# Four seven-product pairs in each half of the long w_down passes, three residues by DMA, and a load queue that follows the buffers

## The chip, the cores and the metric

The kernel runs on one core of one Trainium2 chip. The metric is device time in microseconds (us). Before the change three runs gave 1047.63, 1048.29 and 1048.34 us, so the median is 1048.29 us. Every engine of the core works through its own queue in order: PE multiplies matrices, PEld is the part of PE that loads the standing operand, DVE and ACT do arithmetic on vectors, POOL here does little more than issue DMAs, and SP issues DMAs.

## The reference

One layer of an encoder with sequence 256 and width 2048, all in float32:

```
xn   = rms_norm(x);  q, k, v, ga, gg = split(xn @ w_in)          # w_in 2048 x 5120
att  = differential attention(q, k, v), 4 heads, chunk mask, then rms_norm
u    = silu(layer_norm(causal depthwise conv(ga * sigmoid(gg))))
h    = x + concat(att, u) @ w_out                                 # w_out 2048 x 2048
hn   = rms_norm(h)
out  = h + (silu(hn @ w_gate) * (hn @ w_up)) @ w_down             # 2048 x 5632, twice; 5632 x 2048
```

The last line is some two thirds of the time. It has 5632 hidden columns, which the kernel takes as eleven blocks of 512.

## The kernel before, in words

**Precision.** A float32 number is kept as two parts: a rounded one, `hi`, and what is left, `lo` (the residue). A product of two such numbers takes three matmuls: hi by hi, lo by hi, hi by lo. The rounding is done by ACT (`round_chunk`, L320), the residue by DVE (`split_chunk`, L329). For some chunks the residue is made "by DMA" instead: ACT writes the negative of the raw numbers into `lo` (L323), and POOL issues a DMA that adds the raw numbers in a rounding form onto it (L324).

**Work units.** The last line of the reference runs as a list of chunks, `chunks`. A chunk of kind `g` or `u` (a *two*) covers two tiles of 128 rows and one stretch of 512 columns, and takes 12 matmuls (`multiply_two`, L1014, L1015, L1020). A chunk of kind `s` (a *pair*) covers two tiles of rows and two stretches of columns at once, by the seven products of Strassen's scheme in Winograd's form: 7 x 3 = 21 matmuls where plain work takes 24 (`multiply_pair`, L993 to L995). For a pair the weights must first be combined: `round_pair` makes four sums on DVE (L966 to L968) and rounds the raw ones on ACT (L969); `split_pair` rounds the sums on ACT (L972) and makes the seven residues on DVE (L975, L976). The seven combinations of the other operand are made once (`make_forms` for the gate and up blocks, `make_down_forms` for the passes over w_down).

**Blocks and passes.** Eleven blocks fall in three groups, `FGROUPS = (4, 4, 3)`. A block (but for block 0, which is done plainly) has twelve chunks in the order `ORDER = "sggsggsuusuu"`: 4 pairs and 8 twos. After a group comes its pass over w_down (`down_pass`): two halves, each for 1024 output columns. A pass after four blocks has 16 row tiles; each half takes them as `ND` = 2 pairs and 12 twos, in the orders of `DORDERS[4]`; the short last pass has 12 row tiles, 2 pairs and 8 twos a half. In this text the chunks of a block or a half are called seats 0, 1, 2 and so on.

**Order of the work.** `run_chunks` writes the program in one pass over the chunks: before it writes the matmuls of chunk t it writes the loads and the rounding of chunk t + 3 and the residue of chunk t + 2. The loads of pairs are written six chunks ahead (`PAIR_AHEAD`). Loads go by SP's queue, in the order written, and each waits until its buffer is free: five buffers for twos (`RAW_BUFS`), two for pairs (`wb`). All else (sums of the products, the transposed activations, the combinations for w_down) is written by small generators that are taken one step further at fixed points: four times in a pair, twice in a two (`resume`). `lag(n)` puts n such steps between two parts of a generator.

**The end of a block.** `bank_sums` combines seven PSUM banks on DVE (L1092 to L1099) after the last pair. `block_done` adds the last two banks after the last chunk (L1113), multiplies (L1115), and after a lag of four steps `transposed` has PE transpose the result (L831), ACT round it (L840) and DVE make the residue (L842). In the first two blocks of a group the first two row tiles are kept raw (`raw_act`), for the seven combinations of the pass. `make_down_forms` makes these, one or two instructions every five steps, during the third and fourth block of the group (L868 to L888).

**The end of a half.** `down_half` and `down_whole` add the sums to `hd`, the running sum in memory, by adding DMAs from POOL (L1138, L1155). In the very last half the sums are added on the core and written out.

Of the kernel before, what the change touches and what calls it, by code (L numbers as in the profile page):

```python
# [88 lines left out]
ND = 2  # L89
DORDERS = {4: ("gguuggsguugsuu", "sgggugggusuuuu"), 3: ("gguusggsuu", "gggsgsuuuu")}  # L90
# [8 lines left out]
PAIR_AHEAD = 6  # L99
# [23 lines left out]
def tile_block(  # L123
# [263 lines left out]
    def run_chunks():  # L387
        n = len(chunks)
        i = j = p = 0
        behind = [k for k in range(n) if chunks[k].get("kind") == "s"][NS]  # L390
        for t in range(n):
            hi_lead, lo_lead = lead(t)
            while j < min(i, t + 1 + lo_lead):
                chunks[j]["split"](chunks[j])
                j += 1
            while p < min(n, t + 1 + PAIR_AHEAD):
                if chunks[p].get("kind") == "s":

                    if p < behind and p > t + hi_lead:
                        break  # L400
                    load_pair(chunks[p])
                p += 1
            while i < min(n, t + 1 + hi_lead):
                if i in before:
                    before[i]()
                chunks[i]["load"](chunks[i])
                chunks[i]["round"](chunks[i])
                i += 1
                if hi_lead == lo_lead:
                    chunks[j]["split"](chunks[j])  # L410
                    j += 1
            while j < min(n, t + 1 + lo_lead):
                chunks[j]["split"](chunks[j])
                j += 1
            chunks[t]["multiply"](chunks[t])
# [405 lines left out]
    def transposed(j, aa):  # L821
        last = j + 1 in FIRSTS
        b = j - group_of(j)[1]
        for t in range(N // P // 2):
# [20 lines left out]
            yield from lag(1 if last else 4)  # L845
# [12 lines left out]
    def make_down_forms(g):  # L858

        fp = ffn["pool"]  # L860
        gap = lambda: lag(5 if FGROUPS[g] == 4 else 2)
        a11, a21 = (raw_act[0][:, :, m * P : (m + 1) * P] for m in range(NM))
        a12, a22 = (raw_act[1][:, :, m * P : (m + 1) * P] for m in range(NM))

        hi = fp.tile([P, 7, ND, P], F32R, tag="dhi", name="dhi")
        lo = fp.tile([P, 3, ND, P], F32R, tag="dlo", name="dlo")
        fa, fb = (lhs.tile([P, 2, ND, P], F32, tag=t, name="dsums") for t in ("lhi", "llo"))
        act.copy(hi[:, 0], a11)  # L868
        dve.scalar_tensor_tensor(fa[:, 0], a21, -1.0, a22, ALU.mult, ALU.subtract)
        yield from gap()  # L870
        act.copy(hi[:, 1], a12)
        dve.scalar_tensor_tensor(fa[:, 1], fa[:, 0], -1.0, a11, ALU.mult, ALU.subtract)
        yield from gap()
        act.activation(hi[:, 2], a22, AF.Copy, scale=-1.0)
        dve.tensor_tensor(fb[:, 0], a11, a21, ALU.subtract)
# [8 lines left out]
        dve.scalar_tensor_tensor(lo[:, 2], a22, -1.0, hi[:, 2].bitcast(F32), ALU.mult, ALU.subtract)  # L884
        yield from gap()
        pairs = [lhs.tile([P, 2, ND, P], F32R, tag=t, name="dlo2") for t in ("lhi", "llo")]
        for i, f in ((0, fa), (1, fb)):
            dve.tensor_tensor(pairs[i], f, hi[:, 3 + 2 * i : 5 + 2 * i].bitcast(F32), ALU.subtract)  # L888
            yield from gap()
# [357 lines left out]
```

## Time and profile before

| | us |
|---|---|
| profiled execution, device time | 1048.92 |
| its span on the core | 1047.1 |
| median of three runs | 1048.29 |
| PE busy in the span | 1036.2 |
| DVE busy | 900.6 |
| ACT busy | 621.6 |
| the long pass of the second group, both halves (768.74 to 854.15) | 85.41 |

The span is what the core's instructions cover, and the device time of the same execution is 1.8 us longer. Busy time of PE overlaps itself, because matmuls are pipelined: a matmul is shown with some 0.39 us, while the next one starts 0.23 us after it. Stretches of the span are therefore read by the starts of chunks.

### The profile page before, as it was taken

Reading aid. Unit: us, or ns where it says so; the run is one execution under the profiler, and the core shown is the slowest. Engines: PE = TensorE matmul, PEld = TensorE weight load, DVE = VectorE, ACT = ScalarE, POOL = GpSimd, SP = SyncE. Lnnn points to the kernel's source line nnn. Section 1 sums busy time; section 2 is a strip of 40 time slices with the busy share of each in tenths; the row PEclk is TensorE's granted clock in tenths of the full one; section 3 lists DMA queues with packets and bytes.
Section 4 is the critical chain, followed back from the end, with each engine's and each line's share of the span. In section 5 each row is a group of like instructions: output and inputs, shape, how many; then the busy total and the mean of one; then the engine's idle time right before and its main releaser. Section 6 shows DMA issues by size and latency. Waiting matters only on the chain.

```text
span 1047.1 us, 12933 instructions
## 1 busy us (share of the span) xinstructions
PE 1036.2 (99%) x4663; PEld 852.5 (81%) x4663; DVE 900.6 (86%) x1095; ACT 621.6 (59%) x786; POOL 100.5 (10%) x143
## 2 busy tenths in 40 slices
PE   9999999999999999999999999999999999999998
PEld 7888887877788788888888888888888888888886
DVE  7899889898765599999787898999878789989897
ACT  7544666755756565776463657666644446657442
POOL 0130122201100100000001010000000110000010
PEclk9999999999999999999999999999999999999999
DMA  9657654453546566987867789879757879798683
GB/s 335 227 182 280 212 163 167 154 181 134 177 153 226 194 223 214 268 266 236 232 210 188 217 271 273 256 217 285 248 175 241 219 208 291 222 287 267 187 265 85
DMA packets 113936, 231.30 MB, mean 221 GB/s; under 512 B 7504, under 2 KB 8656, under 8 KB 113616
## 3 DMA queue, kind: packets, MB, share of 16 engines
q1 hardware_dynamic: 104864, 203.71, 56.9%
q0 software_dynamic: 8864, 26.74, 13.4%
q8 instruction: 36, 0.59, 0.2%
q14 instruction: 28, 0.23, 0.1%
q10 hardware_dynamic: 144, 0.03, 0.0%
HBM read 204.24 MB, written 9.44 MB: 204 GB/s over the span
## 4 chain that ended last, share of the span: by engine, by line
PE 61%; DMA 2%; DVE 2%; issue 1%; ACT 0%; DVEq 0%; POOLq 0%
PE q L1020 12%; PE q L1014 12%; PE q L1015 12%; PE q L995 8%; PE q L993 7%; PE q L994 7%; DMA raw<-in_w_down_dram 1%; PE ps_a L831 1%; DMA wlo<-raw 1%; PE acc L365 1%; PE acc L359 1%; PE acc L360 1%; DVE wlo L329 1%; DVE wlt L976 0%; DVE wt L966 0%
## 5 line engine op out<-in xcount | busy, mean ns | idle before, releaser
L320 ACT CAST whi<-raw 128x1024 fp32r<-128x1024 f32 (+1 forms) x273 | 281.5, 1048 | 141.6 <-PE acc L360 58.9
L329 DVE TENSOR_TENSOR wlo<-raw,whi 128x1024 fp32r<-128x1024 f32 (+1 forms) x239 | 287.8, 1218 | 73.5 <-ACT whi L320 73.3
L972 ACT CAST wh<-wt 128x2048 fp32r<-128x2048 f32 x52 | 99.6, 1914 | 77.6 <-DVE wt L968 76.9
L976 DVE TENSOR_TENSOR wlt<-wt,wh 128x2048 fp32r<-128x2048 f32 x52 | 119.1, 2290 | 14.9 <-ACT wh L972 14.7
L359 PE MATMUL acc<-whi,xhi 128*128 128x512 f32 x320 | 126.9, 397 | 1.0 <-ACT whi L320 0.9
L360 PE MATMUL acc<-whi,xlo 128*128 128x512 f32 x320 | 125.2, 391 | 0.0
L1014 PE MATMUL q<-whi,chi 128*128 128x512 f32 x320 | 125.2, 391 | 0.0
L1015 PE MATMUL q<-whi,clo 128*128 128x512 f32 x320 | 124.5, 389 | 0.0
L993 PE MATMUL q<-wh,fhi 128*128 128x512 f32 x280 | 109.9, 393 | 0.0
L994 PE MATMUL q<-wh,flo 128*128 128x512 f32 x280 | 109.1, 390 | 0.0
L517 DVE SCALAR_TENSOR_TENSOR y<-upad,cw,y 128x256 f32<-128x256 f32 x240 | 102.2, 482 | 2.2 <-ACT y L510 2.2
L1014 PE MATMUL q<-whi,ahi 128*128 128x512 f32 x256 | 100.2, 391 | 0.0
L1015 PE MATMUL q<-whi,alo 128*128 128x512 f32 x256 | 99.6, 389 | 0.0
L975 DVE TENSOR_TENSOR wlb<-wb,wh 128x1536 fp32r<-128x1536 f32 x52 | 91.1, 1752 | 1.8 <-ACT wh L969 1.8
L365 PE MATMUL acc<-wlo,xhi 128*128 128x512 f32 x320 | 87.8, 396 | 2.0 <-DVE wlo L329 2.0
L1020 PE MATMUL q<-wlo,chi 128*128 128x512 f32 x320 | 85.7, 390 | 0.2 <-DMA wlo<-raw 0.2
L969 ACT CAST wh<-wb 128x1536 fp32r<-128x1536 f32 x52 | 76.6, 1474 | 0.0
L365 PEld LDWEIGHTS acc<-wlo,xhi 128*128 128x128 f32 x320 | 59.7, 189 | 15.3 <-DVE wlo L329 3.3
L359 PEld LDWEIGHTS acc<-whi,xhi 128*128 128x128 f32 x320 | 60.4, 189 | 14.3 <-ACT whi L320 1.9
L1020 PEld LDWEIGHTS q<-wlo,chi 128*128 128x128 f32 x320 | 59.9, 188 | 13.2 <-DMA wlo<-raw 0.8
L360 PEld LDWEIGHTS acc<-whi,xlo 128*128 128x128 f32 x320 | 60.4, 189 | 12.2
L1014 PEld LDWEIGHTS q<-whi,chi 128*128 128x128 f32 x320 | 60.1, 188 | 12.3
(230 smaller groups left out, 1739.1 us busy)
## 6 DMA issues: line engine op xcount, KB each, us to landing
raw<-in_w_in_dram SPq DMA_DIRECT2D x79, 512.0 KB, 4.6
raw<-in_w_down_dram SPq DMA_DIRECT2D x64, 512.0 KB, 7.2
raw<-in_w_gate_dram SPq DMA_DIRECT2D x48, 512.0 KB, 7.5
raw<-in_w_up_dram SPq DMA_DIRECT2D x48, 512.0 KB, 6.2
wb<-in_w_up_dram SPq DMA_DIRECT2D x40, 512.0 KB, 3.7
wb<-in_w_gate_dram SPq DMA_DIRECT2D x40, 512.0 KB, 4.9
wlo<-raw POOLq DMA_DIRECT2D x34, 512.0 KB, 7.1
raw<-in_w_out_dram SPq DMA_DIRECT2D x32, 512.0 KB, 4.2
```

Of the source, the lines that this page charges most:

```text
L320: act.copy(c["hi"], c["raw"])
L329: dve.tensor_tensor(c["lo"], c["raw"], c["hi"].bitcast(F32), ALU.subtract)
L359: pe.matmul(ps[m], xhi[:, ms], hi[:, j, :], start=c["first"] and j == 0, stop=False)
L360: pe.matmul(ps[m], xlo[:, ms], hi[:, j, :], start=False, stop=False)
L365: pe.matmul(ps[m], xhi[:, ms], lo[:, j, :], start=False, stop=c["last"] and j == nk - 1)
L517: dve.scalar_tensor_tensor(y[:, ct, :], src, wk, y[:, ct, :], ALU.mult, ALU.add)
L976: dve.tensor_tensor(lot, c["t"], c["hi"][:, :SUMMED].bitcast(F32), ALU.subtract)
L993: pe.matmul(ps, hi, c["hi"][:, w], start=bool(first), stop=False)
L994: pe.matmul(ps, lo, c["hi"][:, w], start=False, stop=False)
L1014: pe.matmul(ps, xs[i][0][:, ms], hi[:, i, :], start=i == 0 and bool(c["first"].get(qs[m])), stop=False)
L1015: pe.matmul(ps, xs[i][1][:, ms], hi[:, i, :], start=False, stop=False)
L1020: pe.matmul(sum_bank(c, qs[m]), xs[i][0][:, ms], lo[:, i, :], start=False, stop=i == 1 and bool(c["last"].get(qs[m])))
```

## The change

The passes after four blocks (groups 0 and 1) take four pairs in each half, not two. Their row tiles 0 to 7 go by pairs, 8 to 15 by four twos in each column stretch. Both halves take the order of the gate and up blocks, `ORDER`. In each half three residues of twos are made by DMA and not by DVE: the first and the third `g` (seats 1 and 4) and the second `u` (seat 8). The combinations of the activations are made for four row tiles at a time; all row tiles of the first two blocks of a group are now kept raw. Since the pass now begins with a pair, the transposes of the group's fourth block go where those of other blocks go, with other lags (6 steps before, 3 between). The additions to `hd` are written three steps later. The short last pass keeps its orders and its two pairs.

Loads from the third pair on are no longer written at a fixed lead. As soon as the program has written the residue that is the last reader of a buffer (for a residue by DMA: when it comes to the chunk itself), the load that takes the same buffer next is written; among loads that could be written at the same time the one of the earlier chunk goes first.

```diff
-ND = 2
-DORDERS = {4: ("gguuggsguugsuu", "sgggugggusuuuu"), 3: ("gguusggsuu", "gggsgsuuuu")}
+NDS = (4, 4, 2)
+DORDERS = {4: (ORDER, ORDER), 3: ("gguusggsuu", "gggsgsuuuu")}
+HD_LAG = 3
+DOWN_BY_DMA = {4: (dict(g=(0, 2), u=(1,)),) * 2, 3: (dict(g=(), u=()),) * 2}
...
-PAIR_AHEAD = 6
+PAIR_BUFS = 2
...
     def run_chunks():
         n = len(chunks)
-        i = j = p = 0
-        behind = [k for k in range(n) if chunks[k].get("kind") == "s"][NS]
+        i = j = 0
+        pairs = [k for k in range(n) if chunks[k].get("kind") == "s"]
+        raws = [k for k in range(n) if chunks[k].get("kind") != "s" and not chunks[k].get("spare_raw")]
...
+        ahead = [[k for k in which if k >= pairs[2]] for which in (raws, pairs)]
+        place = [{k: a for a, k in enumerate(which)} for which in (raws, pairs)]
+
+        def freed(side, t):
+            which, bufs = ((raws, RAW_BUFS), (pairs, PAIR_BUFS))[side]
+            if not ahead[side] or pairs[2] - 1 not in loaded:
+                return None
+            k = which[place[side][ahead[side][0]] - bufs]
+            return k if k in split and (t >= k or not chunks[k]["by_dma"]) else None
+
+        def load_freed(t):
+            while True:
+                ready = [(k, side) for side in range(2) if (k := freed(side, t)) is not None]
+                if not ready:
+                    return
+                load(ahead[min(ready)[1]].pop(0))
...
         for t in range(n):
             hi_lead, lo_lead = lead(t)
             while j < min(i, t + 1 + lo_lead):
-                chunks[j]["split"](chunks[j])
+                split_next()
                 j += 1
-            while p < min(n, t + 1 + PAIR_AHEAD):
-                if chunks[p].get("kind") == "s":
-                    if p < behind and p > t + hi_lead:
-                        break
-                    load_pair(chunks[p])
-                p += 1
+            load_freed(t)
...
     def transposed(j, aa):
-        last = j + 1 in FIRSTS
+        last = j + 1 in FIRSTS and NDS[group_of(j)[0]] < HD
...
-            if b < 2 and 2 * t < ND:
-                raw_act[b] = lhs.tile([P, 2, S], F32, tag=("lhi", "llo")[b], name=f"ar{j}")
-                act.copy(raw_act[b], pt)
+            g = group_of(j)[0]
+            nd = NDS[g]
+            if b < 2 and 2 * t < nd:
+                if not b and not t:
+                    raw_act[g] = ffn["pool"].tile([P, 2, nd, S], F32, tag="draw", name="raw_act")
+                act.copy(raw_act[g][:, b, 2 * t : 2 * t + 2, :], pt)
                 yield from lag(3 if last else 6)
-                if b:
-                    start(make_down_forms(group_of(j)[0]))
+                if b and 2 * t + 2 == nd:
+                    start(make_down_forms(g))
                 continue
...
-            yield from lag(1 if last else 4)
+            yield from lag(1 if last else 3 if closing(j) else 4)
+
+    def closing(j):
+        return j + 1 in FIRSTS and NDS[group_of(j)[0]] == HD
...
     def make_down_forms(g):
...
-        act.copy(hi[:, 3:5], fa)
-        dve.tensor_tensor(fb[:, 1], a12, fa[:, 1], ALU.subtract)
+        hs = ffn["pool"].tile([P, 2, nd, P], F32R, tag="dhs", name="dhs")
+        for i, f in ((0, f4), (1, f5)):
+            act.copy(hs[:, i], f)
+        dve.tensor_tensor(f2, a12, f5, ALU.subtract)
         yield from gap()
-        act.copy(hi[:, 5:7], fb)
+        act.copy(hi[3], f2)
         for i, a in ((0, a11), (1, a12)):
-            dve.tensor_tensor(lo[:, i], a, hi[:, i].bitcast(F32), ALU.subtract)
+            dve.tensor_tensor(lo[i], a, hi[i].bitcast(F32), ALU.subtract)
             yield from gap()
...
+        dve.tensor_tensor(lo[3], f2, hi[3].bitcast(F32), ALU.subtract)
+        yield from gap()
+        ls = ffn["pool"].tile([P, 4, nd, P], F32R, tag="draw", name="dls")
+        act.copy(ls[:, 3], f6)
+        for i, (f, h) in enumerate(((f4, hs[:, 0]), (f5, hs[:, 1]), (f6, ls[:, 3]))):
+            dve.tensor_tensor(ls[:, i], f, h.bitcast(F32), ALU.subtract)
+            if i:
+                yield from gap()
...
     def block_done(j, q):
...
-        yield from lag(4)
+        yield from lag(6 if closing(j) else 4)
...
     def down_half(g, n, q, end):
         gs, us = yield from bank_sums(q)
+        if not at_end(g, n):
+            end.update(us=us)
+            yield from lag(HD_LAG)
...
     def down_whole(g, n, q, end):
...
-                pool.dma_start(out=hd[m][:, (n + 1) * N : (n + 2) * N], in_=us[m], accum_op=ALU.add)
                 continue
...
+        if not at_end(g, n):
+            if FGROUPS[g] > 3:
+                yield from lag(HD_LAG)
+            for m in range(NM):
+                pool.dma_start(out=hd[m][:, (n + 1) * N : (n + 2) * N], in_=us[m], accum_op=ALU.add)
```

More of the change, by code (lines that the diff above doesn't have):

```diff
@@ L858, in make_down_forms @@
     def make_down_forms(g):
-        fp = ffn["pool"]
+        nd = NDS[g]
         gap = lambda: lag(5 if FGROUPS[g] == 4 else 2)
[L862 to L867, printed above, removed]
@@ L1080, in down_pass @@
             end = {}
-            fast_block(order, [dict(p=p, rows=slice(k0 + p, k0 + p + HD + 1, HD)) for p in range(ND)], twos,
+            fast_block(order, [dict(p=p, rows=slice(k0 + p, k0 + p + HD + 1, HD)) for p in range(nd)], twos,
                        dict(g=(w_down, n * N), u=(w_down, (n + 1) * N)),
```

62 lines of the change are left out of this document (39 added, 23 removed).

## The prediction

> **What bounds the kernel now.** I read the page's busy times first, then what PE waited for, then the chain of waits, and the timeline at block ends last.
>
> ```profile
> PE 1036.2 (99%) x4663; PEld 852.5 (81%) x4663; DVE 900.6 (86%) x1095; ACT 621.6 (59%) x786; POOL 100.5 (10%) x143
> ```
>
> ```profile
> PE acc L365 <- DVE wlo L329: 2.0, 2, 1.2
> ...
> PE q L1020 <- DMA wlo<-raw: 0.2, 1, 0.2
> PE q L995 <- DVE wlt L976: 0.2, 1, 0.2
> ```
>
> PE is busy 99%, and its waits over the whole run are a few us. Pipelined matmuls can look busy, so the starts must say it:
>
> ```profile
> 546.68 0.91 PE q L1020 x4
> 549.40 0.91 PE q L1020 x4
> 556.88 0.91 PE q L1020 x4
> ```
>
> These chain rows lie in the first long pass. Two to two is 2.72 us, so a matmul costs 2.72 / 12 = 0.2267 us; two to two across a pair is 7.48, so the pair costs 4.76 = 21 x 0.2267. Nothing is lost between them: PE's matmul count is the time. DVE is next:
>
> ```profile
> 685.23:726.99 41.76, 41.76 (x190) 34.56 (x188) 39.00 (x41) 29.18 (x30) 3.48 (x4) 1.00 0.86 252
> 768.74:811.99 43.25, 43.25 (x195) 35.61 (x194) 37.59 (x36) 23.42 (x22) 0.00 (x0) 1.00 0.62 207
> 811.99:854.15 42.16, 42.16 (x187) 34.91 (x186) 33.32 (x33) 19.80 (x18) 5.24 (x6) 1.00 0.75 204
> 854.15:895.05 40.90, 40.90 (x182) 33.71 (x181) 38.08 (x36) 23.05 (x21) 4.34 (x5) 1.00 0.93 289
> ```
>
> The columns are length, then busy time of PE, PEld, DVE, ACT, POOL, the clock (1.00), DMA share and GB/s. The first row is the third block of group 1, the next two are the halves of its pass, the last is the block after it. The block keeps DVE busy 39.0 of 41.76 us and DMA 86%, and PE still runs without a gap; the halves have 5.7 and 8.8 us of DVE to spare.
>
> **The change part by part.** *Matmuls.* A half goes from 2 x 21 + 12 x 12 = 186 to 4 x 21 + 8 x 12 = 180. Four halves: 24 fewer, 24 x 0.2267 = 5.44 us, wholly on the path. The Trainium skill, TensorE: Matmul & The Clock Gate, Part 1, gives 215.7 ns from start to start for 512 columns at full clock; that would make it 5.18 us. The trace shows 226.7 ns and decides.
>
> *DVE in a half.*
>
> ```profile
> L976 DVE TENSOR_TENSOR wlt<-wt,wh 128x2048 fp32r<-128x2048 f32 x4 | 9.2, 2291 | 1.6 <-ACT wh L972 1.6
> L975 DVE TENSOR_TENSOR wlb<-wb,wh 128x1536 fp32r<-128x1536 f32 x4 | 7.0, 1750 | 0.0
> L966 DVE TENSOR_TENSOR wt<-wb 128x1024 f32<-128x1024 f32 x4 | 4.9, 1219 | 0.0
> L329 DVE TENSOR_TENSOR wlo<-raw,whi 128x1024 fp32r<-128x1024 f32 x4 | 4.8, 1219 | 0.0
> L967 DVE TENSOR_TENSOR wt<-wb,wt 128x512 f32<-128x512 f32 x4 | 2.8, 692 | 0.1
> L968 DVE TENSOR_TENSOR wt<-wt,wb 128x512 f32<-128x512 f32 x4 | 2.8, 692 | 0.1
> ...
> L869 DVE SCALAR_TENSOR_TENSOR dsums<-ar,ar 128x256 f32<-128x256 f32 x1 | 0.4, 418 | 0.0
> ```
>
> A pair costs 2.29 + 1.75 + 1.22 + 0.69 + 0.69 = 6.64 us, a residue 1.22. Two more pairs are +13.3; DVE residues go from 12 to 5, -8.5. So +4.8 a half, into 5.7 and 8.8 us of room: hidden on average, but not everywhere (below). The combinations: 9 DVE instructions (seven of 256 elements a partition, 0.42, two of 512, 0.69 as in L968) become 11 of 512, +3.3 a long group, and two residues of activations (L842, 512 elements too) go, -1.4. ACT gains two pairs (1.92 as in L972 below and three quarters of it for the raw weights, 3.4 each) less one cast of a two, about +6 in halves where it is busy 20 to 23 of 42 us: hidden. POOL issues twelve more residue DMAs, 0.87 us each (row at 721.63 below), where it is busy 10%: hidden; but they now stand in one queue with the additions to `hd`, which is a rival below. Should DVE lose its cover, each us over its room is a us of PE, as at the seam that follows.
>
> *The seam from a group's last block to its pass.* Here the change is not hidden. The rows are the seam from the third block to the fourth in group 1, the nearest thing to the new one, since the pass now begins like a block:
>
> ```profile
> 719.40 2.29 DVE L976 TENSOR_TENSOR wlt<-wt,wh 128x2048 fp32r<-128x2048 f32 x1
> 726.73 1.29 DVE L1113 TENSOR_TENSOR sum<-q,sum 128x512 f32<-128x512 f32 x2 [0.55 <-PE q L1020]
> 727.44 0.39 PE L995 MATMUL q<-wlt,fhi 128*128 128x512 f32 x1
> 731.12 0.69 DVE L968 TENSOR_TENSOR wt<-wt,wb 128x512 f32<-128x512 f32 x1
> 732.87 1.92 ACT L972 CAST wh<-wt 128x2048 fp32r<-128x2048 f32 x1
> 734.82 2.29 DVE L976 TENSOR_TENSOR wlt<-wt,wh 128x2048 fp32r<-128x2048 f32 x1 [1.01 <-ACT wh L972]
> 738.10 0.39 PE L995 MATMUL q<-wlt,fhi 128*128 128x512 f32 x1
> 744.71 0.39 PE L1020 MATMUL q<-wlo,chi 128*128 128x512 f32 x1
> 753.89 2.29 DVE L976 TENSOR_TENSOR wlt<-wt,wh 128x2048 fp32r<-128x2048 f32 x1
> 758.99 0.39 PE L995 MATMUL q<-wlt,fhi 128*128 128x512 f32 x1
> ```
>
> The pair of seat 0 is ready at 721.69 and used at 727.44, a lead of 5.75; the pair of seat 3 at 737.11 against 738.10, a lead of 0.99; seat 4 needs its residue at 744.71. In the fourth block the last pair led by 758.99 - 756.18 = 2.81. A block has 33 steps and the parts of the combinations come every five from step 18 of the third block on, so the last three residues now fall late in the fourth: two before the pass's first pair, one just after it. From 2.81, less 0.26 for dearer ones earlier, with PE's 10.2 us (4.76 + 2 x 2.72) for DVE's 1.22 + 2 x 0.69 + 6.64 = 9.2 (some 0.5 less, as rows overlap by 0.08), seat 0 of the pass leads by 3.7 and not 5.75: 2 us late. Set into the seam above, DVE then does 0.6 (the last combination), the bank sums, L1113 and L1115 without the 0.55 wait, the residue of seat 2 (1.15, by DMA in a block), and the sums of seat 3 end not at 731.8 (L968) but at 731.8 + 2.0 + 0.6 + 1.15 - 0.55 = 735.0, less 0.4 for a combination residue that the seam shown has there: 734.6. ACT rounds until 736.5, DVE ends at 738.8: 0.7 late for 738.10.
>
> ACT comes to the residue of seat 4 only after that rounding: cast and negative take 1.9 as the sum of L972 does (both pass 2048 elements a partition), and POOL issues the DMA at 738.4 in the seam's time. It is needed at 744.71, so 6.3 us are left.
>
> ```profile
> DMA to landing us min/median/max: 5.0/7.1/10.2
> 719.44 0.37 SPq L956 DMA_DIRECT2D wb<-in_w_up_dram  x1
> 719.85 0.47 SPq L956 DMA_DIRECT2D wb<-in_w_gate_dram  x1
> 720.42 1.00 SPq L315 DMA_DIRECT2D raw<-in_w_gate_dram  x2
> 721.63 0.87 POOL L324 DMA_DIRECT2D wlo<-raw  x1 [4.86 <-ACT wlo L323]
> DMA to landing us min/median/max: 9.7/9.7/9.7
> ```
>
> The first row is all 34 such DMAs, the last landing row the one issued at 721.63, 2.2 us behind a burst of four loads. So the price is between the 0.7 above (5.0) and 10.2 - 6.3 = 3.9 us of wait. At 738.4 the new queue has let go the pair freed at 736.2 and one raw load, three transfers of 512 KB in place of four: 9.7 less one transfer at the 289 GB/s of the last stretch above (1.8) is 7.9, nearest to my case. 7.9 - 6.3 = 1.6 us, which holds the 0.7. Two passes: +3.2.
>
> *Second halves.* No block ends there; the same reckoning puts the issue 8.2 us before the need. With 7.9 it costs 0; with 10.2, 2.0. Behind the two DMAs of `hd` it could be late (rivals).
>
> *Loads.* They hold up PE nowhere now, so earlier loads save nothing in blocks. At the end of the short pass one pair came late:
>
> ```profile
> 1027.00 0.39 PE L994 MATMUL q<-wh,dlo 128*128 128x512 f32 x1
> 1027.57 0.50 PE L995 MATMUL q<-wlt,dhi 128*128 128x512 f32 x1 [0.18 <-DVE wlt L976]
> ```
>
> 0.57 in place of 0.23 is 0.34 lost; I take -0.4 for such places, between 0 and -0.7. SP's order now follows releases; a load behind a residue by DMA waits for its landing, which comes just before the chunk that PE works on, and the next load has five buffers to come. No cost. The later `hd` additions are needed only a block or half later: 0, and at the end their write-out has over 15 us.
>
> *Sum.* -5.44 + 3.2 + 0 - 0.4 = -2.6 us. The profiled execution took 1048.92 (span 1047.1 and 1.8 around it); it becomes 1046.3. It lay 0.63 above the median, so the median of 1048.29 becomes **1045.6 us**. A measurement of this kernel tells some 0.2%, 2.1 us, from nothing.
>
> **The rivals.** *Nothing comes late.* The new queue sends loads singly, so the residue lands within 6.3 us, as some do (least 5.0), and seat 0 keeps more lead. Then -5.44 - 0.4 = -5.8: 1042.4; to -0.7 at the end, 1042.2. Against it: DMA is 86 to 93% busy in blocks.
>
> *The residue of seat 4 stands behind the `hd` DMAs in second halves.*
>
> ```profile
> DMA to landing us min/median/max: 4.6/5.8/9.5
> ```
>
> The row is that of the ten DMAs of L1138, to `hd`: 5.8 us to land in the median. Four go out around the second half's start, 3 to 9 us ahead of the residue. If the residue takes 9 us in all four halves, first halves cost 9 - 6.3 = 2.7, second ones 0.8, in all 7.0: 1048.29 - 5.84 + 7.0 = 1049.5, no measurable change. The Trainium skill, DMA: Bandwidth & Descriptors, Queues, rings and completion order, has each DMA engine take a queue's descriptors in order and turn about between queues by packets: by it this residue waits behind the `hd` additions of its own queue, and loads on SP's queue only share with it. The 9.7 above, against 5.0, agrees with sharing; no row here shows the first part.
>
> *The same DMA decides for slower.* With latency L the wait is L - 6.3 in first halves and L - 8.2 in second ones, two of each: 4L - 29. It eats the gain of 5.84 at L = 8.7 and makes the kernel slower by 2.1 us at L = 9.2. At the row's worst, 10.2, it is 11.8: 1054.2. For it: the DMA share of the halves rises from 0.62 and 0.75 toward the block's 0.86. Against it: the median of 7.1.
>
> *DVE sets the pace in the passes.* A first half needs 4 x 6.64 + 5 x 1.22 + 5.5 for eight sums + 4 from the block's end (six instructions of 512) = 42.2 us where PE needs 41.7. If seat 0 starts with 1 us of lead and not 3.7, the pair of seat 3 is 3.4 late and later ones do not recover at once: some 4 us a pass, 8 in all, 1050.5.
>
> **How the numbers follow.** My case, 1043.6 to 1046.2: 0.44. Nothing late, below: 0.16. The residue late in all halves, 1046.2 to 1050.4: 0.23. Slower by the worst landing: 0.10; by DVE: 0.07. Faster 0.60, same 0.23, slower 0.17. The range runs from 1042.3 to 1050.2 and leaves the two slower cases out.
>
> **What would show it.** PE has 4639 matmuls and a long pass takes 85.4 - 12 x 0.2267 = 82.7 us and its stalls. The pair of seat 3 in first halves should show a wait on L976 of about 0.7, seat 4 a wait on the residue DMA of about 1; DVE busy is about 900.6 + 4 x 4.8 + 2 x 1.9 = 923.6. I am wrong if PE's waits on that DMA pass 6 us in all, if waits on L976 appear in block after block, or if no wait shows at all.

## The result, and the profile after

The changed kernel takes **1045.94 us** (median of 14 runs, 1045.10 to 1046.68) against 1048.30 for the kernel before on the same chip (14 runs, 1047.63 to 1048.55): 2.36 us less, a ratio of 0.9979 with a 95% interval of 0.9971 to 0.9986. The profiled execution took 1046.62, with a span of 1044.8.

Busy times of the changed kernel, and what its PE waited for (total us, how often, longest):

```profile
PE 1031.2 (99%) x4639; PEld 847.9 (81%) x4639; DVE 924.0 (88%) x1109; ACT 645.3 (62%) x804; POOL 110.7 (11%) x155
```

```profile
PE q L1038 <- DVE wlt L1019: 1.5, 3, 0.7
...
PE q L1063 <- DMA wlo<-raw: 1.0, 2, 0.6
```

There are 24 matmuls fewer, as the change says. In the part that was changed two waits grew, that on the residues of a pair (L1019, L976 before) and that on a residue by DMA, each 0.2 us before. A third, of PE on ACT's first roundings, grew from 0.9 to 1.8, but it lies in the first 11 us of the kernel. The stretches of its second long pass, and the landing of all its 46 residues by DMA, answer to the rows shown of before:

```profile
767.50:810.20 42.70, 42.04 (x189) 34.48 (x188) 40.86 (x41) 28.93 (x26) 3.05 (x4) 1.00 0.87 257
810.20:852.00 41.80, 41.16 (x182) 33.75 (x181) 37.12 (x34) 23.55 (x19) 5.38 (x8) 1.00 0.94 257
...
DMA to landing us min/median/max: 5.4/7.0/9.7
```

DVE has 1.8 us to spare in the first half and 4.7 in the second, where it had 5.7 and 8.8, and the share of the DMA engines went from 0.62 and 0.75 to 0.87 and 0.94. In the lines of the changed kernel a pair is L1036 to L1038, a two L1057, L1058 and L1063, the residue by DMA L326.

To see where the time lies I take, chunk by chunk, the distance from one first matmul to the next, less 0.2267 a matmul and 0.45 for four transposes. What is left is called lost. From the first block of pairs to the last two the kernel before spends 649.22 us, 2.8 of them such losses; the changed one 646.61, of which 5.6. The difference, -2.61, is -5.44 of matmuls and +2.83 of losses. Almost all the new losses lie at two places of each long pass. The first, in the pass of group 0 (starts of seats 3, 4 and 5, what they waited for, and the transposes inside seat 3):

```profile
527.62 0.39 PE L1036 MATMUL q<-wh,dhs 128*128 128x512 f32 x1
528.88 0.50 PE L1038 MATMUL q<-wlt,dhs 128*128 128x512 f32 x1 [0.65 <-DVE wlt L1019]
531.28 0.60 PE L861 MATMUL ps_a<-ident,sum 128*128 128x128 f32 x4
533.81 0.39 PE L1057 MATMUL q<-whi,ahi 128*128 128x512 f32 x1
535.81 1.21 PE L1063 MATMUL q<-wlo,ahi 128*128 128x512 f32 x4
536.86 0.40 PE L1057 MATMUL q<-whi,ahi 128*128 128x512 f32 x1
```

Seat 3 takes 6.19 in place of 4.76 + 0.45, so 0.98 is lost; seat 4 takes 3.05 in place of 2.72, 0.33. In group 1 it is 1.01 and 0. The second place is seat 4 of the second half:

```profile
574.97 0.39 PE L1057 MATMUL q<-whi,ahi 128*128 128x512 f32 x1
577.26 1.19 PE L1063 MATMUL q<-wlo,ahi 128*128 128x512 f32 x4 [0.32 <-DMA wlo<-raw]
578.29 0.40 PE L1057 MATMUL q<-whi,ahi 128*128 128x512 f32 x1
```

3.32 for 2.72: 0.60 lost, of which the row names 0.32. It counts from the end of the matmul before, which is drawn 0.16 beyond the next regular start, and the four matmuls behind the wait take 1.03 (577.26 to 578.29) and not 0.91. In group 1 the loss is 0.92. That makes 2.32 in first halves and 1.52 in second ones. Against it 1.0 went: 0.54 at a residue in the first product block, and four losses of about 0.13 at seats 3 and 6 of the old passes. The short pass's end still loses 0.20 and 0.54, where it lost 0.24 and 0.47.

### The profile page after: what moved, and what is told of

The parts are those of the page before. It is cut to its first block, busy times and chain, and to the rows that moved or that the text cites. A ratio compares the mean times of both kernels' runs of the same rounds, so it can differ in the third digit from the quotient of the medians.

```text
span 1044.8 us, 12991 instructions
## 1 busy us (share of the span) xinstructions
PE 1031.2 (99%) x4639; PEld 847.9 (81%) x4639; DVE 924.0 (88%) x1109; ACT 645.3 (62%) x804; POOL 110.7 (11%) x155
## 4 chain that ended last, share of the span: by engine, by line
PE 52%; DVE 8%; issue 2%; DMA 2%; ACT 1%; DVEq 0%; ACTq 0%
PE q L1057 9%; PE q L1058 9%; PE q L1063 9%; PE q L1038 8%; PE q L1036 7%; PE q L1037 7%; DMA wlo<-raw 2%; DVE wlo L331 1%; DVE wlt L1019 1%; DVE wt L1009 1%; PE acc L367 1%; ACT wh L1015 1%; PE acc L361 1%; PE acc L362 1%; PE ps_a L861 1%
## 5 line engine op out<-in xcount | busy, mean ns | idle before, releaser
L322 ACT CAST whi<-raw 128x1024 fp32r<-128x1024 f32 (+1 forms) x257 | 265.2, 1047 | 101.9 <-PE acc L362 58.9
L331 DVE TENSOR_TENSOR wlo<-raw,whi 128x1024 fp32r<-128x1024 f32 (+1 forms) x211 | 254.3, 1216 | 51.2 <-ACT whi L322 50.5
L1015 ACT CAST wh<-wt 128x2048 fp32r<-128x2048 f32 x60 | 114.9, 1915 | 108.8 <-DVE wt L1011 108.7
L1019 DVE TENSOR_TENSOR wlt<-wt,wh 128x2048 fp32r<-128x2048 f32 x60 | 137.4, 2290 | 19.5 <-ACT wh L1015 19.4
L1057 PE MATMUL q<-whi,chi 128*128 128x512 f32 x320 | 125.2, 391 | 0.0
L1058 PE MATMUL q<-whi,clo 128*128 128x512 f32 x320 | 124.5, 389 | 0.0
L1036 PE MATMUL q<-wh,fhi 128*128 128x512 f32 x280 | 109.9, 392 | 0.0
L1018 DVE TENSOR_TENSOR wlb<-wb,wh 128x1536 fp32r<-128x1536 f32 x60 | 105.0, 1751 | 1.0 <-ACT wh L1012 1.0
L326 POOL DMA_DIRECT2D wlo<-raw x46 | 39.8, 864 | 505.8 <-ACT wlo L325 272.1
L1012 ACT CAST wh<-wb 128x1536 fp32r<-128x1536 f32 x60 | 88.4, 1474 | 0.0
L1063 PE MATMUL q<-wlo,chi 128*128 128x512 f32 x320 | 85.5, 389 | 0.0
L1057 PE MATMUL q<-whi,ahi 128*128 128x512 f32 x192 | 74.9, 390 | 0.0
L1058 PE MATMUL q<-whi,alo 128*128 128x512 f32 x192 | 74.7, 389 | 0.0
L1009 DVE TENSOR_TENSOR wt<-wb 128x1024 f32<-128x1024 f32 x60 | 73.1, 1218 | 0.0
```

The lines of the kernel that those rows point to most:

```text
L322: act.copy(c["hi"], c["raw"])
L331: dve.tensor_tensor(c["lo"], c["raw"], c["hi"].bitcast(F32), ALU.subtract)
L1015: act.copy(c["hi"][:, :SUMMED], c["t"])
L1019: dve.tensor_tensor(lot, c["t"], c["hi"][:, :SUMMED].bitcast(F32), ALU.subtract)
L1036: pe.matmul(ps, hi, c["hi"][:, w], start=bool(first), stop=False)
L1057: pe.matmul(ps, xs[i][0][:, ms], hi[:, i, :], start=i == 0 and bool(c["first"].get(qs[m])), stop=False)
```

## The experiments

All are edits of the changed kernel but one. Its own figure stands first.

| run | median, us | runs | ratio to before, interval |
|---|---|---|---|
| the changed kernel | 1045.94 | 14 | 0.9979 (0.9971 to 0.9986) |
| early_forms | 1049.44 | 11 | 1.0012 (1.0003 to 1.0021) |
| seats_12 | 1044.08 | 5 | 0.9961 (0.9948 to 0.9975) |
| hd_late | 1046.46 | 11 | 0.9981 (0.9973 to 0.9990) |
| seats_12_early | 1048.87 | 11 | 1.0004 (0.9995 to 1.0013) |
| early_step | 1044.40 | 5 | 0.9961 (0.9947 to 0.9974) |
| hd_soon | 1046.27 | 11 | 0.9981 (0.9972 to 0.9989) |
| old_loads | 1063.89 | 4 | 1.0150 (1.0136 to 1.0164) |
| loads_alone (edit of the kernel before) | 1048.27 | 11 | 0.9998 (0.9989 to 1.0006) |
| mixed | 1044.06 | 5 | 0.9961 (0.9947 to 0.9974) |
| mixed_tail | 1043.89 | 5 | 0.9957 (0.9945 to 0.9970) |
| hd_none | 1044.96 | 6 | 0.9970 (0.9958 to 0.9981) |
| dve_all | 1050.65 | 9 | 1.0025 (1.0015 to 1.0034) |

Executions of one kernel differ by 1 to 3 us here. Each kernel has one profile only, so why they differ isn't shown. Part of it may lie ahead of all that was changed: in the profiles the first block of pairs starts anywhere from 390.2 to 391.3 us. One profile shows where that execution loses; how much a kernel loses on the whole is told by the medians.

### early_forms: combinations closer together

```diff
-        gap = lambda: lag(5 if FGROUPS[g] == 4 else 2)
+        gap = lambda: lag(4 if FGROUPS[g] == 4 else 2)
```

> The changed kernel with the combinations for the long passes made one step closer together: one or two instructions every four steps, not every five, so that the last three residues of them come some 15 us earlier, inside the fourth block. My theory: the pair of seat 3 in the first halves is late (0.98 and 1.01 us in the changed kernel's chain) because the lead of the pass's seat 0 has fallen to 3.56 us, and it has fallen because three of these residues (0.69 each) fall between the last pair of the block and the pass. Then seat 0 leads by 5 us or more, seat 3 loses less than 0.2 in each pass, and seat 4, whose cast follows on ACT, loses nothing: -2.0 to -2.3 us against the changed kernel's 1045.94, about 1043.8. Rival 1: DVE is short of time over the whole stretch, and not only at these places; then the work comes earlier but the stall moves to another pair in the fourth block or the half, and the time stays within 0.5 us. Rival 2: the two units of the raw residue of seat 2 (1.22 on DVE) are what makes seat 3 late; then seat 3 still loses 0.3 or more.

Measured: 3.5 us slower than the changed kernel, where 2.0 to 2.3 less were expected. A wait that nobody had foreseen stands first in what PE waited for:

```profile
PE q L1058 <- DVE alo L875: 3.5, 2, 1.7
```

Seat 3 lost 0.46 and 0.03 where it had lost 0.98 and 1.01, but seat 5 lost 2.04 and 2.08, waiting for the residue of the last two row tiles of activations. On DVE, in the changed kernel and then in this one:

```profile
533.59 0.68 DVE L875 TENSOR_TENSOR alo<-ps_a,ahi 128x512 fp32r<-128x512 f32 x1
534.19 1.75 DVE L1018 TENSOR_TENSOR wlb<-wb,wh 128x1536 fp32r<-128x1536 f32 x1
535.86 2.28 DVE L1019 TENSOR_TENSOR wlt<-wt,wh 128x2048 fp32r<-128x2048 f32 x1
```

```profile
533.40 1.75 DVE L1018 TENSOR_TENSOR wlb<-wb,wh 128x1536 fp32r<-128x1536 f32 x1
535.52 2.29 DVE L1019 TENSOR_TENSOR wlt<-wt,wh 128x2048 fp32r<-128x2048 f32 x1 [0.37 <-ACT wh L1015]
537.73 0.69 DVE L875 TENSOR_TENSOR alo<-ps_a,ahi 128x512 fp32r<-128x512 f32 x1
```

The residue has slipped behind seven residues of a pair, 4 us. The code says why: `multiply_pair` takes an extra step as long as the combinations are not there (`while (fs := c["pairs"]()) is None: resume()`). In the changed kernel the last combination is not written when the pass's first pair is, so one step is taken there, and the transposes come a step earlier for it; with the combinations made earlier that step is gone. So far this was only argued; early_step tests it. Also, the lead of seat 0 (the time from the end of its residues to their first use) grew little, to 3.64 and 4.06 in the two passes from 3.56: DVE has hardly any idle time before it, so work done earlier makes the pairs before it less early (1.44 and 1.36 for 2.56 at the last pair of the block).

### seats_12: residues of seats 1 and 2 by DMA, not 1 and 4

```diff
-DOWN_BY_DMA = {4: (dict(g=(0, 2), u=(1,)),) * 2, ...
+DOWN_BY_DMA = {4: (dict(g=(0, 1), u=(1,)),) * 2, ...
```

> The changed kernel with the residues of seats 1, 2 and 8 by DMA in the halves of the long passes, in place of seats 1, 4 and 8: as many as before, with the second one earlier. DVE makes the residue of seat 4 and is rid of that of seat 2, which stands ahead of the pair of seat 3. My theory: in first halves the 1.0 us of seat 3 goes, since 1.22 us of DVE is taken from in front of it; in second halves seat 4's wait for the DMA (0.60 and 0.92) goes, since DVE makes it; the 0.33 of the first half goes too. In all 3.8 us of stalls go, and what may come back is a wait for seat 2's DMA: it is issued some 10 us ahead of its use by my reckoning and lands in 5 to 9. So 1042.2 to 1043.0. Rival: seat 2's DMA is late in place of seat 4's: then a wait on the residue DMA of 0.5 to 2 us shows at seat 2 in all four halves, and the time stays at 1044.5 to 1047.

Measured: 1044.08, 1.9 us less than the changed kernel where 2.9 to 3.7 were expected. In its profile the losses at seat 3 and at seat 4 of both halves are gone, as they should be if the residue of seat 2 on DVE and the DMA of seat 4 stood behind them. But seat 2 waits in the first halves, 0.31 and 1.29. The second of these, with the issue of its DMA:

```profile
769.86 0.86 POOL L326 DMA_DIRECT2D wlo<-raw  x1 [6.71 <-ACT wlo L325]
```

```profile
776.37 1.20 PE L1063 MATMUL q<-wlo,ahi 128*128 128x512 f32 x4 [0.98 <-DMA wlo<-raw]
```

It went out 5.3 us before its use and not the 10 I had reckoned, because ACT's part of it (L325) came late, and took 6.5. That is the rival, in first halves only.

### seats_12_early: both edits

```diff
-DOWN_BY_DMA = {4: (dict(g=(0, 2), u=(1,)),) * 2, ...
+DOWN_BY_DMA = {4: (dict(g=(0, 1), u=(1,)),) * 2, ...
-        gap = lambda: lag(5 if FGROUPS[g] == 4 else 2)
+        gap = lambda: lag(4 if FGROUPS[g] == 4 else 2)
```

> Both edits at once: the residues of seats 1, 2 and 8 by DMA, and the combinations every four steps. If each takes away another part of the seam's loss, the sum of both gives about 1042.2 to 1042.6, which is the case in which nothing comes late in the long passes. If both take away the same microsecond (seat 3's, 2.0 us in all), the time is that of the better one of the two, less at most 0.3. If the residue of seat 2 is late by DMA, this kernel stays at 1044 or more, and the edit of the combinations alone is the faster one.

Measured: 1048.87. Only the expectation's last case (1044 or more) leaves room for that, and not for its reason: seat 2 loses 0.34 in group 0 and nothing in group 1. The 2.05 at seat 5 of both first halves is there again, with the same wait on L875. Seat 3 loses nothing.

### early_step: the step put back

```diff
-        gap = lambda: lag(5 if FGROUPS[g] == 4 else 2)
+        gap = lambda: lag(4 if FGROUPS[g] == 4 else 2)
...
-        yield from lag(6 if closing(j) else 4)
+        yield from lag(5 if closing(j) else 4)
```

> The changed kernel with the combinations every four steps, as in the run early_forms, and with the lag before the transposes of a group's fourth block at 5 steps and not 6. Theory: early_forms was slower for a reason that has nothing to do with the combinations' price. In the changed kernel they are not finished when the program comes to the pass's first pair, so the program takes one extra step there, and with it the transposes come one step (1.2 us) earlier; made earlier, they need no extra step, the transposes slip by it, and the residue of the second two row tiles falls behind the pair of seat 6 on DVE, which cost 2.05 at seat 5 in each pass. With the lag at 5 the transposes are back at their step: seat 5 loses nothing, seat 3 loses 0.5 or less in each pass in place of 1.0, seat 4 nothing. Against the changed kernel's 1045.94: -0.9 to -1.4, so 1044.5 to 1045.0. Rival: the 2.05 at seat 5 is the price of DVE work that is only moved about; then seat 5 or another seat of the first half still loses 1 us or more and the time is 1047 or above.

Measured: 1044.40, 5.0 us faster than early_forms by one step, and 1.5 faster than the changed kernel, a little more than expected (their intervals, 0.9947 to 0.9974 and 0.9971 to 0.9986, just touch). Seat 5 loses nothing; seat 3 loses 0.55 and nothing, seat 4 of the first halves 0.27 and nothing. So the slip was the cause of the 2.05. With the last combination residue (0.69) no longer between the residues of seat 0 and those of seat 3 on DVE, half of seat 3's loss goes in group 0 and all of it in group 1, where seat 0 also leads by 4.17 and not 3.56. The second halves keep their loss at seat 4, 0.31 and 1.62, and the last residue by DMA of group 1's fourth block lands 0.6 late.

### hd_late, hd_soon, hd_none: the additions to hd

hd_late writes them behind the residue of seat 4 of the second half, hd_soon takes the lag of three away, hd_none leaves those out that stand ahead of that residue, so that its result lacks them.

```diff
-HD_LAG = 3
+HD_LAG = 9
...
-            yield from lag(HD_LAG)
+            yield from lag(HD_LAG if FGROUPS[g] > 3 else 3)
```

> The changed kernel with the additions to hd of the long passes written nine steps after their sums and not three, so that POOL issues those of a first half's end behind the residue of seat 4 of the second half. Nothing else is moved. Theory A: that residue takes 8.2 and 8.6 us to land, against 7.0 and 5.4 in first halves, because the two or four hd DMAs stand ahead of it in POOL's queue. Then it lands in 5.5 to 7 us, the stalls of 0.60 and 0.92 at seat 4 of the second halves go, and the time falls by 1.3 to 1.5 us, to 1044.5. Theory B: the latency comes from the loads of SP that are under way at the same time; then it stays at 8 to 9 us and so does the time, within 0.4 us. If the hd DMAs only share the engines, they cost the same from behind as from ahead, which is B's result too.

```diff
-HD_LAG = 3
+HD_LAG = 0
```

> The changed kernel without the three steps by which the additions to hd are put off; they go out some 3.5 us earlier, as before the change. Theory A (the residue of seat 4 in second halves lands late because the hd DMAs are in front of it in POOL's queue and still under way): they now have 11 us and not 8 before that residue is issued, so it lands in 6.5 to 7.5 us where it took 8.2 and 8.6, and the stalls of 0.60 and 0.92 shrink to 0.3 or less: -0.9 to -1.5, about 1044.7. Theory B (it is SP's loads at that time): the residue keeps 8 us or more and the time stays within 0.4 of 1045.94. If A is right but an hd DMA needs 10 us and more to land, the gain is half of that.

```diff
+            if FGROUPS[g] > 3 and n == 0:
+                continue
             if not at_end(g, n):
                 pool.dma_start(out=hd[m][:, cs], in_=gs[m], accum_op=ALU.add)
...
-            for m in range(NM):
+            for m in range(NM if FGROUPS[g] < 4 or n else 0):
                 pool.dma_start(out=hd[m][:, (n + 1) * N : (n + 2) * N], in_=us[m], accum_op=ALU.add)
```

> The changed kernel without the four additions to hd at the end of the first half of each long pass (so the output lacks the first 1024 columns of those two passes); their eight DMAs are what stands ahead of the residue of seat 4 in the second halves. The sums on DVE stay. Theory A (those DMAs delay the residue): it lands in 6 to 7 us as in the run hd_late (6.4 and 6.9), not in 8.2 and 8.6; the stalls of 0.60 and 0.92 go, and with nothing put in their place elsewhere the time falls by 1.2 to 1.6 us, to 1044.3 to 1044.7. Theory B (SP's loads do it, and hd_late moved something else): it still takes 8 us or more and the time stays within 0.4 of 1045.94.

Time: 1046.46, 1046.27 and 1044.96. Only hd_none gains, 1.0 of the 1.2 to 1.6 expected, and its interval (0.9958 to 0.9981) overlaps that of the changed kernel; in its one profile the product part is only 0.3 shorter (646.3 for 646.6). hd_soon decided nothing: its additions went out at the same time as before. The rows are the additions and the last of the sums on DVE, in the changed kernel and then in hd_soon:

```profile
559.08 0.68 DVE L1143 TENSOR_TENSOR sum<-q,sum 128x512 f32<-128x512 f32 x1
559.76 1.74 POOL L1185 DMA_DIRECT2D hd<-sum  x2 [3.24 <-issue]
```

```profile
558.76 0.68 DVE L1143 TENSOR_TENSOR sum<-q,sum 128x512 f32<-128x512 f32 x1
559.45 1.74 POOL L1185 DMA_DIRECT2D hd<-sum  x2 [3.24 <-issue]
```

In both they go out as the sums end. In group 1 the rows of both kernels name these sums as what POOL waited for (L1142, 3.00). So the lag of three steps was not what set their time.

The landings tell more. For the residue of seat 4 I count the DMAs that had been issued before it and had not landed when it was issued:

| kernel | half | in flight, groups 0 and 1 | lands after, us |
|---|---|---|---|
| changed | first | 2, 2 | 7.0, 5.4 |
| changed | second | 6, 6 | 8.2, 8.6 |
| hd_soon | second | 6, 6 | 8.2, 8.4 |
| early_step | second | 6, 7 | 8.0, 9.3 |
| hd_late | second | 3, 2 | 6.4, 6.9 |
| hd_none | second | 3, 2 | 8.6, 5.5 |
| old_loads (below) | first | 4, 4 | 11.6, 11.6 |
| old_loads | second | 7, 6 | 8.6, 8.3 |

The six in the changed kernel are two additions, two raw loads and the two loads of a pair (the landing lines are those of the pair's loads and of the residue at 568.98):

```profile
560.85 2.41 POOL L1212 DMA_DIRECT2D hd<-sum  x2
562.08 0.95 SPq L317 DMA_DIRECT2D raw<-in_w_down_dram  x2
566.46 0.88 SPq L999 DMA_DIRECT2D wb<-in_w_down_dram  x2
568.98 0.89 POOL L326 DMA_DIRECT2D wlo<-raw  x1 [5.72 <-ACT wlo L325]
```

```profile
DMA to landing us min/median/max: 10.6/10.9/11.2
...
DMA to landing us min/median/max: 8.2/8.2/8.2
```

In hd_late the same pair of loads lands in 5.2 and 6.0 us, and of the raw loads one has landed when the residue is issued and the other lands 0.2 us later:

```profile
DMA to landing us min/median/max: 5.2/5.6/6.0
...
DMA to landing us min/median/max: 6.4/6.4/6.4
```

The loads of the pair show it in both groups: 10.2 to 11.8 us with the additions ahead (the changed kernel), 4.1 to 7.7 without (hd_late and hd_none). The residue lands sooner in three of the four places without them. So the additions delay the loads, and in three places of four the residue: theory A and B seem to be one backlog. Put behind the residue, the additions let it land in time (its two losses are gone in the profile of hd_late), but then they take 8.8 to 14.1 us themselves, and the median shows no gain. Where that was lost I did not settle; the one execution profiled, the fastest of the eleven, has new losses of 0.55, 0.27 and 0.25 in blocks. The fourth place speaks against the backlog as the whole cause: in hd_none the residue of group 0 took 8.6 with only three DMAs ahead, and its seat lost 0.97, more than the 0.60 with the additions. In group 1 seat 4 lost nothing, but seat 8 of the first half lost 0.62. What delays a residue besides is open.

### old_loads and loads_alone: the load queue

old_loads is the changed kernel with the loads of the kernel before; loads_alone is the reverse.

```diff
-PAIR_BUFS = 2
+PAIR_AHEAD = 6
...
-            load_freed(t)
+            while p < min(n, t + 1 + PAIR_AHEAD):
+                ...
```

> The changed kernel with the loads written as before the change: pairs six chunks ahead, twos with their rounding. My theory, on which the prediction took 7.9 us and not 9.7 for the residue of seat 4: behind bursts of four loads a residue by DMA lands later than behind single ones. Then the residues of seats 4 and 8 in the passes take 8.5 to 9.7 us, the stalls at seat 4 grow by 1 to 2 us in each half where they can, and the first product block gets its 0.54 back: +2 to +5 us, 1048 to 1051. Rival: the order of the loads doesn't matter to them; the latencies stay at 5.4 to 8.6 in the passes and the time is within 0.7 of the changed kernel's 1045.94.

> The kernel before with nothing but the new load queue. By my sum the loads bring little by themselves: the wait for a residue of 0.54 in the first product block goes (as it went in the changed kernel), the two late pairs in the short pass (0.24 and 0.47) stay, as they did in the changed kernel. So -0.3 to -0.6: 1047.7 to 1048.0. Rival: the new queue is what made the changed kernel faster; then this one comes to 1046.5 or less, and the four pairs a half bring nothing. A third way: by the interval no difference from 1048.30 at all, with the 0.54 gone in the first block and as much lost elsewhere.

loads_alone: 1048.27, no difference. The 0.54 in the first product block went, and 0.50 and 0.21 came at two other seats: the third way. old_loads: 1063.89, 18 us slower than the changed kernel. The direction was right, the size over three times the most that I gave. Its waits, the four loads ahead of seat 4's residue (issued at 530.10), and what became of that (a two is L1029, L1030 and L1035 in this kernel):

```profile
PE q L1035 <- DMA wlo<-raw: 12.0, 7, 4.7
```

```profile
527.60 0.88 SPq L971 DMA_DIRECT2D wb<-in_w_down_dram  x2
528.58 0.93 SPq L317 DMA_DIRECT2D raw<-in_w_down_dram  x2
```

```profile
536.71 0.39 PE L1030 MATMUL q<-whi,alo 128*128 128x512 f32 x1
541.79 2.08 PE L1035 MATMUL q<-wlo,ahi 128*128 128x512 f32 x4 [4.69 <-DMA wlo<-raw]
543.66 0.63 PE L1029 MATMUL q<-whi,ahi 128*128 128x512 f32 x1
544.09 0.63 PE L1030 MATMUL q<-whi,alo 128*128 128x512 f32 x1
```

With four loads of 512 KB sent 1.0 to 2.5 us ahead of it the residue takes 11.6 us and not 7.0. Seats 4 and 5 lose 7.1 and 7.3 in the two first halves; most of the rest is spread over other residues by DMA. The second halves have the same four loads, sent as shortly before, and two or three additions besides, and there the residue takes 8.6 and 8.3. So the number of DMAs under way does not give the price alone; what makes the first halves dearer is open. The kernel before had no residue by DMA in its passes, so its bursts cost little there. The queue is worth nothing by itself and is the condition for the rest.

### dve_all: no residue by DMA in the long passes

```diff
-DOWN_BY_DMA = {4: (dict(g=(0, 2), u=(1,)),) * 2, ...
+DOWN_BY_DMA = {4: (dict(g=(), u=()),) * 2, ...
```

> The changed kernel with no residue by DMA in the long passes: DVE makes all eight of each half. My sum has DVE at 40.9 of 43.0 us in a first half and 37.1 of 41.5 in a second one; three residues of 1.22, rows overlapping by 0.08, add 3.4 to each. That is 44.3 in a first half, over what PE needs there (42.2), and 40.5 in a second one (40.8). So first halves lose 1 to 1.5 us more than the 1.3 and 1.0 they lose now, most of it at the pair of seat 3, second halves lose the 0.60 and 0.92 no more: 0 to +2.5 us against the changed kernel, 1046 to 1048.5. Rival 1: DVE has no such slack anywhere; then each half loses the whole 3.4 and the time is 1056 or more. Rival 2: the DMAs are not needed at all; then the time is 1045.9 or less.

Measured: 1050.65, 4.7 us slower than the changed kernel, more than my 0 to 2.5 and far from the rival's 10. Its waits, and the two halves of group 0 (columns as in the prediction's table of stretches):

```profile
PE q L1038 <- DVE wlt L1019: 6.4, 7, 1.6
```

```profile
517.00:560.00 43.00, 41.41 (x186) 33.73 (x185) 41.58 (x40) 25.97 (x23) 0.00 (x0) 1.00 0.61 201
560.00:602.00 42.00, 41.08 (x182) 33.67 (x181) 40.29 (x37) 21.33 (x17) 3.50 (x4) 1.00 0.80 232
```

First halves lose 2.02 and 2.01 at seat 3, 1.0 more, as reckoned. I had put second halves down as just enough; they lose 1.23 at their seat 3 too, and the block behind loses 0.9 at its seat 3. Room in a half taken as a mean is not room at its first seats: seat 0 of the second half of group 0 leads by 3.1 us and not by 4.9 as in the changed kernel, and the losses end only behind the block's seat 3.

### mixed and mixed_tail: what can be had

mixed is early_step with seats 1, 2 and 8 by DMA in second halves only; mixed_tail moves the last pair of the short pass one seat back besides.

```diff
-DOWN_BY_DMA = {4: (dict(g=(0, 2), u=(1,)),) * 2, ...
+DOWN_BY_DMA = {4: (dict(g=(0, 2), u=(1,)), dict(g=(0, 1), u=(1,))), ...
```

```diff
-... 3: ("gguusggsuu", "gggsgsuuuu")}
+... 3: ("gguusggsuu", "gggsugsuuu")}
```

> The changed kernel with the combinations every four steps and the lag at 5 (as in early_step), and in the second halves of the long passes alone the residues of seats 1, 2 and 8 by DMA (as in seats_12), while the first halves keep seats 1, 4 and 8. By my theory the stalls add up by places: first halves as in early_step (0.81 in group 0, 0 in group 1), second halves as in seats_12 (none, where early_step lost 0.31 and 1.62). So 1.9 us less than early_step's 1044.40: 1042.3 to 1043.2, the fastest of all so far. Rival: what a residue by DMA gains at one place it takes from the next residues of the queue; then a stall of 0.5 to 1.5 shows at seat 8 or in the block behind, and the time is that of early_step or seats_12, 1043.9 to 1044.6.

> The run mixed with the short pass's last half in another order: its second pair at seat 6 and a u two at seat 5, in place of the reverse. Theory: that pair is late for DVE (0.52 lost, lead 0.05) because it stands two seats behind the pair of seat 3; one two more between them is 2.72 us, more than DVE lacks. So its 0.5 goes and nothing else moves: -0.4 to -0.6 against mixed. Rival: the bank sums behind the last pair come 2.72 us later with three and not four twos left to cover them, and the end of the kernel behind the last matmul grows by up to that; then it is 0 to 2 us slower than mixed.

mixed: 1044.06, no faster than early_step or seats_12, as its rival said. In its profile the halves are as expected (0.46 at one seat 3, nothing else), but two residues of blocks come late, 0.54 and 0.73. mixed_tail: 1043.89, 0.17 less than mixed. In its profile the loss of 0.5 at the short pass's last pair is gone, as it should be if DVE held that pair, and the first of the two late residues loses 1.05 and not 0.54; 0.17 between medians of five runs with a scatter of 1.5 to 2.3 shows nothing. mixed_tail is the fastest version found, 2 us under the changed kernel; their intervals (0.9945 to 0.9970, 0.9971 to 0.9986) do not meet.

## Why the prediction held, point by point

The median was put at 1045.6 and came to 1045.94. The sum, -2.6, is that of the trace (-2.61 in the product part), but that it fits so closely is luck: three of its terms were off, by -0.9 (first halves), +1.5 (second halves) and -0.6 (losses that went), and made up for each other.

- **Matmuls, -5.44:** right. 4639 of them, and the second long pass takes 84.47 us (767.48 to 851.95), 82.7 and its stalls of 1.9 within 0.2.
- **DVE:** 923.6 predicted, 924.0 measured. The last pair's lead of 2.81 less 0.26 came out (2.56). For seat 0 the terms as given add up to 3.5, or 4.0 with the half us for overlap, and not to the 3.7 taken; measured 3.56. The seam, moved by 767.48 - 726.99 = 40.49: the sums of seat 3 were to end at 734.6 and ended at 775.09 (734.60), DVE at 738.8 and at 779.36 (738.87). The rows that carry it:

```profile
774.40 0.69 DVE L1011 TENSOR_TENSOR wt<-wt,wb 128x512 f32<-128x512 f32 x1
775.01 1.75 DVE L1018 TENSOR_TENSOR wlb<-wb,wh 128x1536 fp32r<-128x1536 f32 x1
777.07 2.29 DVE L1019 TENSOR_TENSOR wlt<-wt,wh 128x2048 fp32r<-128x2048 f32 x1 [0.31 <-ACT wh L1015]
```

- **First halves, +3.2:** measured 2.32. The 0.7 of seat 3 was right (0.65 in the row, 1.0 by the starts). Too dear was the residue of seat 4: 7.9 us taken, 7.0 and 5.4 measured.
- **Second halves, 0: the step that failed.** Measured 1.52. I gave 8.2 us of room and took the same 7.9 for the landing; the room was 7.8 (568.98 to 574.97 + 1.81), the landing 8.2 and 8.6. It was the place that the rival of the `hd` DMAs named, with about its price of 0.8 each. I priced both halves by one row, picked by the loads alone, although two additions and four loads were under way in one and two loads in the other. The row of 5.8 us shown for the additions was that of L1138 alone; the other ten, of L1155, to which the two under way here belong (L1212 now), took this in the kernel before:

```profile
DMA to landing us min/median/max: 5.0/8.8/11.8
```

- **Loads, -0.4 at the short pass's end:** wrong place. Nothing was gained there (the loss of that pair went when mixed_tail gave DVE more time); 1.0 was gained elsewhere. Half of that is the 0.54 in the first product block, and loads_alone, which has it too, lost 0.7 at two other seats.
- **Later additions to hd, 0:** probably too cheap, and part of the step above; without the four at the end of each long pass's first half the median falls by 1.0, by intervals that overlap.
- **DVE as the pace:** not in this kernel, but near. Three residues more a half make it so (dve_all).

The Trainium skill, DMA: Bandwidth & Descriptors, Queues, rings and completion order, has each DMA engine serve its queues in turns, and has the descriptors of one ring taken in order, though a later one may finish its write first. The landings agree with the first part: the residue that took 8.2 lands 0.9 us before the second of the two loads that SP had issued ahead of it. They don't contradict the second, which the Trainium skill states for the queues of SP and ACT: the additions land before the residue where they stand ahead of it (the changed kernel) and behind it where they stand behind (hd_late). As they were issued 7.6 us before it in the first case, that doesn't show the order. Neither part gives the price.

## What to carry to other kernels

Price a DMA place by place, by the landings nearest to that place, and not by the median of its kind: the same 512 KB took 5.4 us with two loads ahead and 11.6 with four fresh ones. What is under way when it is issued is the first thing to look at, but not the whole price, as the 8.6 and 8.3 with six or seven DMAs ahead show. Where two edits come together, try each alone and each left out: the load queue alone was worth nothing, and without it the other part was 15.5 us slower than no change at all. And where steps are counted, look for loops that take a step while they wait: making something earlier took such a step away and cost 5 us at another place.

## What the runs showed of the hardware that was not expected

A stall of PE of some 5 us costs more than itself. After the 4.69 us at 541.79 in old_loads the matmuls start 0.427 us apart (543.66 to 544.09 above), and not 0.2267, for some ten matmuls, and the granted clock is 0.57 over that stretch (the columns are length, PE busy, clock, DMA share, GB/s):

```profile
541.70:547.00 5.30, 5.21 (x14) 0.57 0.84 292
547.00:553.00 6.00, 6.00 (x28) 1.00 0.97 255
```

Seats 4 and 5 lose 7.1 and 7.3 where the stalls themselves are 4.9 and 4.8, so some 2.2 to 2.5 us come on top of each. The waits of up to 1.6 us in dve_all left the clock at 1.00 (its rows above). The Trainium skill, TensorE: Matmul & The Clock Gate, Part 1, has the array fall to half its clock after an idle window of about 3.4 us and gives 426.7 ns a matmul of 512 columns then. The trace agrees with the second figure (0.427); not quite with the first: the clock falls at 539.4, 2.3 us after the end of PE's last matmul (536.71 + 0.39), and in group 1 after 2.9.

Second, with the same two loads under way the residue of seat 4 in first halves landed in 6.2 to 7.2 us in group 0 and in 5.3 to 5.6 in group 1, in each of the six kernels changed, hd_soon, hd_late, hd_none, early_step and mixed. What makes that difference is open; it wasn't tried.
